# A hybrid decoder step on one core: order of a unit's half products, and raw weight blocks loaded one by one

## The chip, the cores and the metric

The kernel runs on one core of a Trainium2 chip. The time is device time in microseconds (us), from a run on the chip; a run that is profiled as well leaves a trace, from which all rows below come. Matrix products run on TensorE (PE), element-wise work on VectorE (DVE) and ScalarE (ACT), stores are issued from GpSimd (POOL) and nearly all loads from SyncE (SP).

## What is computed

One layer of a hybrid decoder on 1024 new tokens and on 8 single tokens with a state. A combined input projection feeds a gated linear recurrence and a chunked matrix-memory head group; both are merged and projected back. Cut to what matters here:

```
hn = rmsnorm(x, g_norm)                       # (1024, 1024) and (8, 1024)
u = hn @ w_in                                 # w_in (1024, 7176)
xa, za, uq, uk, uv, uo, zb, ui, uf = jnp.split(u, SPLIT_IDX, axis=-1)
yA, hA, bufA = rglru_branch(xa, ...)
hB, C, n, m = mlstm_seq(q, k, v, ig, lf, C0, n0, m0)
...
merged = jnp.concatenate([yA * silu(za), yB * silu(zb)], axis=-1)
x = x + merged @ w_out
y = rmsnorm(x, g_final)
```

The change touches the way in which `u = hn @ w_in` is worked through.

## The kernel before

**Units.** The columns of `w_in` are taken in 14 units of two blocks of 256 columns each (`UNITS`: v0v1, x0y0, q0k0, ... z2z3). Unit 0 is multiplied plainly at the start. For units 1 to 13 the product is a 2 x 2 block product with seven multiplications in place of eight (a Strassen-Winograd scheme): tokens in two halves, the 1024 rows of `w_in` in two halves (b = 0, 1), columns in two blocks (a = 0, 1). `blk(u, a, b)` is one of the four raw weight blocks of a unit; the seven left factors (`cb`) are built once. The products are named by position: `Q_P1, Q_P2, Q_P5, Q_P6, Q_P7, Q_P3, Q_P4 = range(7)`. In the prediction, "first factor" is the weight factor of Q_P1, "second" that of Q_P2, and so on to "seventh", that of Q_P7.

**A product and its halves.** `product(u, q)` makes two half products (s = 0, 1), each of 128 output columns, or, for v and o units, of 256 tokens. Each is a sum of float32 products in three passes (`mm3`, lines 66 to 68: high by high, high by low, low by high): 12 matmuls of 512 columns, or 24 of 256 columns for v and o. Products 1, 6, 7 and 4 add up in one PSUM tile X (tag `kv`, 2 buffers), products 2, and then 5 and 3, in a tile Y (tag `o`, 3 buffers). After each half `evac` reads out: after 1, X is copied by ACT (line 328); after 2, DVE adds Y to the copy (line 331) and the result is stored; 5 (line 335) and 6 (line 338) are copied; 7 (line 341) and 3 (line 345) are added; 4 is copied (line 353) and stored.

**The weight factors.** `prep(u, q)` turns a raw block, or a sum of blocks, into a high and a low part: ACT casts (line 72, `wh`), DVE subtracts (line 73, `wl`). Blocks are summed in place by DVE: at Q_P5 `blk(0,0)` loses `blk(1,0)` (line 279) and `blk(1,0)` gains `blk(1,1)` (line 280); at Q_P6 `blk(1,0)` becomes `blk(1,1) - blk(0,0)` (line 282), and `blk(0,1)` loses it after the split (line 288). The last readers are therefore: of `blk(1,0)` Q_P6, of `blk(0,0)` Q_P7, of `blk(0,1)` Q_P3, of `blk(1,1)` Q_P4. Splits run two products ahead (`LEAD = 2`), in six buffers (`NWS = 6`, three pairs of high and low), so a split can begin when the product three before it has ended. At Q_P5, `dec_unit` first multiplies the 8 single tokens by all four blocks (line 257, 64 small matmuls per unit).

**The raw blocks.** Two tiles of 1 MB (`raw0` for b = 0, `raw1` for b = 1), one buffer each. `load_raw(u, b)` makes a new tile for the unit and issues two loads of 512 KB from SP (line 243), one per column block. The next unit's b = 0 is loaded after Q_P7's split, b = 1 after Q_P4's.

**Beside the products.** Three lists of small steps (`bg`, `rgq`, `dcq`: gates, the recurrence, the single tokens' state, the first chunks of the head group) are popped after each half product by `pop_bg`. In the last unit, `wo_due(q)` puts the steps for the output weights on `bg` after each product. Then comes the second large stage, the output products (`r_prod`) between the chunks.

**What sets the order.** The program text gives priorities. A planner builds each engine's queue at build time: it goes through the instructions with estimated durations and places on each engine the first in program order of those that are ready by its clock. So an instruction can stand ahead of one that is asked for earlier. On the chip each queue runs in its fixed order, and instructions wait on semaphores.

Of the kernel before, what the change touches and what calls it, by code (L numbers as in the profile page):

```python
# [9 lines left out]
F32 = mybir.dt.float32  # L10
# [12 lines left out]
NH = 4  # L23
# [28 lines left out]
def hymba_kernel(  # L52
# [11 lines left out]
    def mm3(out, ah, al, bh, bl, first, last):  # L64

        TE.matmul(out, ah, bh, start=first, stop=False, skip_group_check=True)  # L66
        TE.matmul(out, ah, bl, start=False, stop=False, skip_group_check=True)  # L67
        TE.matmul(out, al, bh, start=False, stop=last, skip_group_check=True)  # L68
# [13 lines left out]
    def ps(tag, shape):  # L82
        return psp.tile(shape, F32, tag=tag, name=f"ps_{tag}", bufs=NBUF.get(tag, 1))
# [17 lines left out]
    def sg(shape, name, dt=F32):  # L101

        return stg.tile(shape, dt, tag="stg", name=name)
# [130 lines left out]
    def load_raw(u, b, parts=(0, 1)):  # L234

        if u >= len(units):
            return
        if (u, b) not in raws:
            raws[u, b] = rawp.tile([P, 4, 512], F32, tag=f"raw{b}", name=f"raw{b}_{u}")
        for a in parts:  # L240
            kind, j = units[u][a]
            c = COL[kind] + j * 256
            ld(raws[u, b][:, :, a * 256:(a + 1) * 256],
               w_in[0, b * HT:(b + 1) * HT, c:c + 256].rearrange("(k p) c -> p k c", p=P))
# [24 lines left out]


    wops = {}

    def blk(u, a, b):
        return raws[u, b][:, :, a * 256:(a + 1) * 256]

    def prep(u, q):
        if q == Q_P5:
            dec_unit(u)
            V.tensor_tensor(blk(u, 0, 0), blk(u, 0, 0), blk(u, 1, 0), op=ALU.subtract)
            V.tensor_tensor(blk(u, 1, 0), blk(u, 1, 0), blk(u, 1, 1), op=ALU.add)  # L280
        if q == Q_P6:
            V.tensor_tensor(blk(u, 1, 0), blk(u, 1, 1), blk(u, 0, 0), op=ALU.subtract)
        src = {Q_P1: (0, 0), Q_P2: (0, 1), Q_P5: (1, 0), Q_P6: (1, 0), Q_P7: (0, 0), Q_P3: (0, 1), Q_P4: (1, 1)}
        hi, lo = ws([P, 4, 256], f"wh{u}_{q}"), ws([P, 4, 256], f"wl{u}_{q}")
        split(hi, lo, blk(u, *src[q]))
        wops[u, q] = hi, lo
        if q == Q_P6:
            V.tensor_tensor(blk(u, 0, 1), blk(u, 0, 1), blk(u, 1, 0), op=ALU.subtract)
        b = {Q_P7: 0, Q_P4: 1}.get(q)
        if b is not None:  # L290
            if u + 1 < len(units):
                load_raw(u + 1, b)
            else:
                if b == 1:
                    r_open(0)

    px = {}

    def product(u, q):

        kind = units[u][0][0]
        wh, wl = wops.pop((u, q))
        bh, bl = cb[q]
        first, last = q in (Q_P1, Q_P2, Q_P5), q in (Q_P2, Q_P3, Q_P4)
        for s in range(2):
            if q == Q_P1:
                px["X", s] = ps("kv", [P, 512])
            if q in (Q_P2, Q_P5):
                px["Y", s] = ps("o", [P, 512])
            X, Y = px["X", s], px.get(("Y", s))  # L310
            out = X if q in (Q_P1, Q_P6, Q_P7, Q_P4) else Y
            if kind in "vo":
                for i in range(2):
                    t = slice((2 * s + i) * P, (2 * s + i + 1) * P)
                    for k in range(4):
                        mm3(out[:, i * 256:(i + 1) * 256], bh[:, k, t], bl[:, k, t], wh[:, k, :], wl[:, k, :],
                            first and i == 0 and k == 0, last and i == 1 and k == 3)
            else:
                c = slice(s * P, (s + 1) * P)
                for k in range(4):  # L320
                    mm3(out, wh[:, k, c], wl[:, k, c], bh[:, k, :], bl[:, k, :], first and k == 0, last and k == 3)
            evac(u, q, s, X, Y)
            yield

    def evac(u, q, s, X, Y):
        if q == Q_P1:
            px["s1", s] = t = sg([P, 512], "s1")
            A.copy(t, X)
        elif q == Q_P2:
            t = px.pop(("s1", s))  # L330
            V.tensor_tensor(t, t, Y, op=ALU.add)
            emit_out(u, 0, 0, s, t)
        elif q == Q_P5:
            px["s5", s] = t = sg([P, 512], "s5")
            A.copy(t, Y)
        elif q == Q_P6:
            px["s2", s] = t = sg([P, 512], "s2")
            A.copy(t, X)
        elif q == Q_P7:
            t = px.pop(("s5", s))  # L340
            V.tensor_tensor(t, t, X, op=ALU.add)
            emit_out(u, 1, 1, s, t)
        elif q == Q_P3:
            t = px.pop(("s2", s))
            V.tensor_tensor(t, t, Y, op=ALU.add)
            emit_out(u, 0, 1, s, t)
        else:
            t = sg([P, 512], "c21")
            o = units[u][1][0] == "o"
            if o:  # L350
                A.activation(t, X, AF.Tanh, scale=0.5)
            else:
                A.copy(t, X)
            emit_out(u, 1, 0, s, t, o)
# [7 lines left out]
    def emit_out(u, a, b, s, t, done=False):  # L362

        kind, j = units[u][a]
        if kind in "xy":
            if a == 1:
                silu2(t)
            stq((d_x, d_y)[a][2 * j + s][:, b * HT:(b + 1) * HT], t)
            return
        if kind in "qk":  # L370
            stq(d_qk[j][(kind == "k") * 2 + s][:, b * HT:(b + 1) * HT], t)
            return
        if kind == "z":
            silu2(t)
            stq(d_zs[2 * j + s, :, b * HT:(b + 1) * HT], t)
            return
        if kind == "o" and not done:
            A.activation(t, t, AF.Tanh, scale=0.5)
        d = {"v": d_v, "o": d_so}[kind][j]
        t0 = b * HT + s * 256  # L380
        stq(d[t0:t0 + 256, :].rearrange("(i p) c -> p i c", p=P), t.rearrange("p (i c) -> p i c", i=2))
# [554 lines left out]
    def dec_rows(half):  # L936

        pvd = ps("s", [NB, 512])
        for m in range(4):
            TE.transpose(pvd[:, m * P:(m + 1) * P], dv[:, 4 * half + m, :], idF)  # L940
        vr = sg([NB, 512], "vr")
        V.tensor_copy(vr, pvd)
        for h in range(2):
            stq(d_dv[2 * half + h], vr[:, h * 256:(h + 1) * 256])
# [457 lines left out]
    def r_open(n):  # L1402

        rring.append(rawp.tile([P, 4, HT], F32, tag="raw1", name="ring0") if n == 0 else slot(5, "ring1", F32))
        for i in range(2 * n, 4):
            r_fetch(4 * n + i)
# [256 lines left out]
            step(Q_P7)  # L1663


    seq = [(u, q) for u in range(1, len(units)) for q in range(7)]
    state = {"prep": 0, "m": False}

    def preps(n):
        while state["prep"] < min(n, len(seq)):  # L1670
            prep(*seq[state["prep"]])
            state["prep"] += 1

    gg = gates()
    bg.extend([lambda: next(gg, None)] * 17 + [rd_open])
    last_u = len(units) - 1
    unit_of = {p: u for u, pair in enumerate(units) for p in pair}
    done_h = [max(unit_of[k, h] for k in "qkv") for h in range(NH)]

    def m_start():  # L1680
        state["m"] = True
        bg.append(m_open1)
        for n in range(NH):
            bg.extend(m_first(n))

    preps(LEAD)
    part = 0
    for n, (u, q) in enumerate(seq):
        preps(n + 1 + LEAD)
        for _ in product(u, q):  # L1690
            pop_bg(2 if u == 1 or u == last_u else 1, 1, part % DEC[1 if u >= DEC[0] else 2] == 1)
            part += 1
        if u == last_u:
            wo_due(q)
        if q == 6:
            for kind, j in units[u]:
                if kind == "x":
                    rg_unit(j)
            for half in range(2):
                if u == max(unit_of["v", 2 * half], unit_of["v", 2 * half + 1], 1):  # L1700
                    bg.append(lambda half=half: dec_rows(half))
            for h in range(NH):
                if done_h[h] == u:
                    bg.append(lambda h=h: dcq.extend(decode_steps(h)))
            if u == last_u - 1:
                dgen = decode_outputs()

                def step():
                    next(dgen, None)
                    run_late()  # L1710
                state["out"] = [step] * 5 + [m_open2]
        if not state["m"] and u > max(done_h) and not (bg or rgq or dcq or late):
            m_start()
        if u == last_u and q == 0:
            if not state["m"]:
                while bg or rgq or dcq or late:
                    pop_bg()
                m_start()
            bg.extend(state["out"])
    while bg or late:  # L1720
        pop_bg()
    with tc.issue_after(lastt[0].ins):
# [102 lines left out]
```

## Time and profile before

| | |
|---|---|
| median of 3 runs | 915.67 us (915.23 to 915.72) |
| the profiled execution | 913.23 us, of which its span 911.3 us |
| granted TensorE clock | 0.999 |
| PE, DVE, ACT busy | 899.6, 739.3, 585.0 us |
| raw block loads (line 243) | 55 loads of 512 KB |

The span runs from the first to the last instruction of the program; a small part of an execution lies around it. Busy times are unions of an engine's instructions; PEld is the loading of matmul weights, which lies beside the matmuls. In a row of the time line the columns are start and duration in us, engine, line of the kernel, operation, output tile, input tiles, shapes and count; in brackets the idle time before it and what ended it. In a row of waits: what waited, for what, us in total, times, longest.

### The profile page before, as it was taken

To read this page: it belongs to the slowest core of one execution; us is meant where nothing else is said; L and a number is where in the kernel's file an instruction comes from. 1 tells how busy PE (TensorE), PEld (TensorE's weight loads), DVE (VectorE), ACT (ScalarE), POOL (GpSimd) and SP (SyncE) were. 2 spreads that over 40 slices of the span, in tenths; PEclk is the share of its full clock that TensorE was granted. 3 is DMA by queue.
4 is the path that set the end of the run, shared out by engine and by line. 5 is a ranking of instruction groups with operands and counts; after the bars stand their busy time and mean duration, and the time that the engine had idled before them with its cause. 6 is when DMAs were issued, how large, how long until landed. Compare 5 with 4: busy or idle time off the path is not lost. (4 is left out here: it accounts for less than half of the span.)

```text
span 911.3 us, 16738 instructions
## 1 busy us (share of the span) xinstructions
PE 899.6 (99%) x5889; PEld 762.3 (84%) x5889; DVE 739.3 (81%) x1528; ACT 585.0 (64%) x1086; POOL 194.2 (21%) x322
## 2 busy tenths in 40 slices
PE   8999999999999999999999999999999999999996
PEld 6997778877788997887789999887788888888886
DVE  6974778979698978789889876679998879888973
ACT  7653446867567776576658775446786568566642
POOL 1111112122222232324332334010111111121120
PEclk9999999999999999999999999999999999999999
DMA  6412447465746566548665747345679888855531
GB/s 200 149 64 92 139 147 250 135 205 187 236 128 221 171 203 204 197 145 266 201 237 184 253 139 244 108 133 191 215 234 259 202 216 296 217 142 180 181 124 67
DMA packets 130493, 167.76 MB, mean 184 GB/s; under 512 B 17596, under 2 KB 98564, under 8 KB 130402
## 3 DMA queue, kind: packets, MB, share of 16 engines
q1 hardware_dynamic: 108790, 103.68, 37.4%
q0 software_dynamic: 21616, 63.02, 20.9%
q8 instruction: 46, 0.75, 0.3%
q14 instruction: 37, 0.30, 0.1%
q10 hardware_dynamic: 4, 0.00, 0.0%
HBM read 108.00 MB, written 62.92 MB: 188 GB/s over the span
## 5 line engine op out<-in xcount | busy, mean ns | idle before, releaser
L72 ACT CAST wh<-raw 128x1024 fp32r<-128x1024 f32 x91 | 95.4, 1049 | 79.5 <-DVE raw L280 21.0
L73 DVE TENSOR_TENSOR wl<-raw,wh 128x1024 fp32r<-128x1024 f32 x91 | 111.1, 1221 | 29.4 <-ACT wh L72 15.8
L66 PE MATMUL ps_kv<-cb_hi,wh 128*128 128x512 f32 x320 | 127.4, 398 | 0.0
L68 PE MATMUL ps_kv<-cb_hi,wl 128*128 128x512 f32 x320 | 125.5, 392 | 0.0
L67 PE MATMUL ps_kv<-cb_lo,wh 128*128 128x512 f32 x320 | 125.2, 391 | 0.0
L66 PE MATMUL ps_o<-cb_hi,wh 128*128 128x512 f32 x240 | 95.2, 397 | 0.0
L68 PE MATMUL ps_o<-cb_hi,wl 128*128 128x512 f32 x240 | 93.7, 391 | 0.0
L67 PE MATMUL ps_o<-cb_lo,wh 128*128 128x512 f32 x240 | 93.6, 390 | 0.0
L66 PEld LDWEIGHTS ps_kv<-cb_hi,wh 128*128 128x128 f32 x320 | 60.1, 188 | 15.9 <-issue 3.1
L68 PEld LDWEIGHTS ps_kv<-cb_hi,wl 128*128 128x128 f32 x320 | 60.1, 188 | 13.4 <-issue 0.6
L67 PEld LDWEIGHTS ps_kv<-cb_lo,wh 128*128 128x128 f32 x320 | 60.1, 188 | 12.7 <-issue 0.8
L66 PE MATMUL ps_kv<-wh,cb_hi 128*128 128x256 f32 x192 | 55.1, 287 | 0.0
L67 PE MATMUL ps_kv<-wl,cb_hi 128*128 128x256 f32 x192 | 54.4, 283 | 0.0
L68 PE MATMUL ps_kv<-wh,cb_lo 128*128 128x256 f32 x192 | 54.3, 283 | 0.0
L66 PEld LDWEIGHTS ps_o<-cb_hi,wh 128*128 128x128 f32 x240 | 45.1, 188 | 10.4 <-issue 0.8
L68 PEld LDWEIGHTS ps_o<-cb_hi,wl 128*128 128x128 f32 x240 | 45.0, 188 | 9.9
L66 PE MATMUL ps_o<-wo,mh 128*128 128x512 f32 (+1 forms) x136 | 53.0, 390 | 0.0
L67 PEld LDWEIGHTS ps_o<-cb_lo,wh 128*128 128x128 f32 x240 | 45.1, 188 | 8.9
L68 PE MATMUL ps_o<-wo,ml 128*128 128x512 f32 (+1 forms) x136 | 51.6, 380 | 0.0
L67 PE MATMUL ps_o<-wo,mh 128*128 128x512 f32 (+1 forms) x136 | 51.5, 379 | 0.0
L66 PE MATMUL ps_o<-wh,cb_hi 128*128 128x256 f32 x144 | 41.0, 284 | 0.0
L67 PE MATMUL ps_o<-wl,cb_hi 128*128 128x256 f32 x144 | 40.7, 283 | 0.0
(559 smaller groups left out, 2603.8 us busy)
## 6 DMA issues: line engine op xcount, KB each, us to landing
raw<-in_w_in_dram SPq DMA_DIRECT2D x55, 512.0 KB
Cb<-in_state_mlstm_C_dram SPq DMA_DIRECT2D x32, 256.0 KB
out_dram<-Cb POOLq DMA_DIRECT2D x32, 256.0 KB, 4.9
qk<-d_qk SPq DMA_DIRECT2D x32, 256.0 KB
ring<-d_ro SPq DMA_DIRECT2D x26, 256.0 KB
d_qk<-s POOLq DMA_DIRECT2D x24, 256.0 KB, 4.8
d_x<-s POOLq DMA_DIRECT2D x16, 256.0 KB, 2.8
zsr<-d_y SPq DMA_DIRECT2D x16, 256.0 KB
```

Source lines behind the costliest of these rows:

```text
L66: TE.matmul(out, ah, bh, start=first, stop=False, skip_group_check=True)
L67: TE.matmul(out, ah, bl, start=False, stop=False, skip_group_check=True)
L68: TE.matmul(out, al, bh, start=False, stop=last, skip_group_check=True)
L72: a = A.copy(hi, src)
L73: V.tensor_tensor(lo, src, hi.bitcast(F32), op=ALU.subtract)
```

## The change

The halves become the unit of order. In units 1 to 12 the second product comes ahead of the first; in the last unit the first stays ahead. Then 5 and 6 as before, the first half of 3, both halves of 7, the second half of 3, and 4. The splits follow the order 2, 1, 5, 6, 7, 3, 4 (1, 2, ... in the last unit), at the halves listed in `PREP`. Whichever of products 1 and 2 is read out first is copied by ACT, the other added by DVE.

One raw tile per b serves all units, and each block of the next unit is loaded on its own, after its last reader's split: `blk(1,0)` after Q_P6, `blk(0,0)` after Q_P7, `blk(0,1)` after Q_P3, `blk(1,1)` after Q_P4. The steps of `wo_due` are put on the list after the halves listed in `DUE`.

```
         if (u, b) not in raws:
-            raws[u, b] = rawp.tile([P, 4, 512], F32, tag=f"raw{b}", name=f"raw{b}_{u}")
+            raws[u, b] = raws[0, b] if (0, b) in raws else rawp.tile([P, 4, 512], F32, tag=f"raw{b}", name=f"raw{b}")
...
+    FREED = {Q_P6: (0, (1,)), Q_P7: (0, (0,)), Q_P3: (1, (0,)), Q_P4: (1, (1,))}
...
-        b = {Q_P7: 0, Q_P4: 1}.get(q)
-        if b is not None:
-            if u + 1 < len(units):
-                load_raw(u + 1, b)
-            else:
-                if b == 1:
-                    r_open(0)
+        if u + 1 < len(units):
+            if q in FREED:
+                load_raw(u + 1, *FREED[q])
+        elif q == Q_P4:
+            r_open(0)
...
-    def product(u, q):
+    def product(u, q, s):
...
-        wh, wl = wops.pop((u, q))
+        wh, wl = wops.pop((u, q)) if s == 1 else wops[u, q]
...
-        if q == Q_P1:
-            px["s1", s] = t = sg([P, 512], "s1")
-            A.copy(t, X)
-        elif q == Q_P2:
-            t = px.pop(("s1", s))
-            V.tensor_tensor(t, t, Y, op=ALU.add)
-            emit_out(u, 0, 0, s, t)
+        if q in (Q_P1, Q_P2):
+            Z = X if q == Q_P1 else Y
+            if ("s1", s) not in px:
+                px["s1", s] = t = sg([P, 512], "s1")
+                A.copy(t, Z)
+            else:
+                t = px.pop(("s1", s))
+                V.tensor_tensor(t, t, Z, op=ALU.add)
+                emit_out(u, 0, 0, s, t)
...
-    seq = [(u, q) for u in range(1, len(units)) for q in range(7)]
+    last_u = len(units) - 1
+    FIRST = lambda u: (Q_P1, Q_P2) if u == last_u else (Q_P2, Q_P1)
+    seq = [(u, q) for u in range(1, len(units)) for q in (*FIRST(u), *range(2, 7))]
...
+    REST = [(Q_P5, 0), (Q_P5, 1), (Q_P6, 0), (Q_P6, 1), (Q_P3, 0), (Q_P7, 0), (Q_P7, 1), (Q_P3, 1), (Q_P4, 0), (Q_P4, 1)]
+    PREP = 0, 2, 4, 6, 8, 11, 12
+    DUE = 1, 3, 5, 7, 10, 12, 13
+
     preps(LEAD)
     part = 0
-    for n, (u, q) in enumerate(seq):
-        preps(n + 1 + LEAD)
-        for _ in product(u, q):
+    for u in range(1, len(units)):
+        for n, (q, s) in enumerate([(q, s) for q in FIRST(u) for s in range(2)] + REST):
+            if n in PREP:
+                preps(7 * (u - 1) + PREP.index(n) + 1 + LEAD)
+            product(u, q, s)
             pop_bg(2 if u == 1 or u == last_u else 1, 1, part % DEC[1 if u >= DEC[0] else 2] == 1)
             part += 1
-        if u == last_u:
-            wo_due(q)
-        if q == 6:
+            if u == last_u and n in DUE:
+                wo_due(DUE.index(n))
+            if n == 13:
...
-        if not state["m"] and u > max(done_h) and not (bg or rgq or dcq or late):
+            if n % 2 and not state["m"] and u > max(done_h) and not (bg or rgq or dcq or late):
...
-        if u == last_u and q == 0:
+            if u == last_u and n == 1:
```

The number of matmuls, casts, sums, loads and stores is the same before and after.

More of the change, by code (lines that the diff above doesn't have):

```diff
@@ L301, in product @@
         kind = units[u][0][0]
-        wh, wl = wops.pop((u, q))
+        wh, wl = wops.pop((u, q)) if s == 1 else wops[u, q]
         bh, bl = cb[q]
         first, last = q in (Q_P1, Q_P2, Q_P5), q in (Q_P2, Q_P3, Q_P4)
-        for s in range(2):
-            if q == Q_P1:
[L307 to L317, printed above, removed]
-            else:
[L319 to L323, printed above, removed]
@@ L325, in evac @@
-    def evac(u, q, s, X, Y):
-        if q == Q_P1:
-            px["s1", s] = t = sg([P, 512], "s1")
-            A.copy(t, X)
-        elif q == Q_P2:
-            t = px.pop(("s1", s))
-            V.tensor_tensor(t, t, Y, op=ALU.add)
-            emit_out(u, 0, 0, s, t)
+        if q == Q_P1:
+            px["X", s] = ps("kv", [P, 512])
+        if q in (Q_P2, Q_P5):
+            px["Y", s] = ps("o", [P, 512])
+        X, Y = px.get(("X", s)), px.get(("Y", s))
+        out = X if q in (Q_P1, Q_P6, Q_P7, Q_P4) else Y
@@ new lines, in product @@
+        if kind in "vo":
+            for i in range(2):
+                t = slice((2 * s + i) * P, (2 * s + i + 1) * P)
+                for k in range(4):
+                    mm3(out[:, i * 256:(i + 1) * 256], bh[:, k, t], bl[:, k, t], wh[:, k, :], wl[:, k, :],
+                        first and i == 0 and k == 0, last and i == 1 and k == 3)
+        else:
+            c = slice(s * P, (s + 1) * P)
+            for k in range(4):
+                mm3(out, wh[:, k, c], wl[:, k, c], bh[:, k, :], bl[:, k, :], first and k == 0, last and k == 3)
@@ L333, in evac @@
+        evac(u, q, s, X, Y)
+    def evac(u, q, s, X, Y):
+        if q in (Q_P1, Q_P2):
[3 more added lines that the diff above has]
+                A.copy(t, Z)
+            else:
+                t = px.pop(("s1", s))
+                V.tensor_tensor(t, t, Z, op=ALU.add)
+                emit_out(u, 0, 0, s, t)
         elif q == Q_P5:
@@ L1675, in hymba_kernel @@
     bg.extend([lambda: next(gg, None)] * 17 + [rd_open])
-    last_u = len(units) - 1
     unit_of = {p: u for u, pair in enumerate(units) for p in pair}
@@ L1691, in hymba_kernel @@
             pop_bg(2 if u == 1 or u == last_u else 1, 1, part % DEC[1 if u >= DEC[0] else 2] == 1)
             part += 1
-        if u == last_u:
-            wo_due(q)
-        if q == 6:
[L1696 to L1711, printed above, removed]
@@ L1712, in hymba_kernel, with step @@
-        if not state["m"] and u > max(done_h) and not (bg or rgq or dcq or late):
-            m_start()
-        if u == last_u and q == 0:
-            if not state["m"]:
-                while bg or rgq or dcq or late:
-                    pop_bg()
-                m_start()
-            bg.extend(state["out"])
+            if u == last_u and n in DUE:
+                wo_due(DUE.index(n))
+            if n == 13:
+                for kind, j in units[u]:
+                    if kind == "x":
+                        rg_unit(j)
+                for half in range(2):
+                    if u == max(unit_of["v", 2 * half], unit_of["v", 2 * half + 1], 1):
+                        bg.append(lambda half=half: dec_rows(half))
+                for h in range(NH):
+                    if done_h[h] == u:
+                        bg.append(lambda h=h: dcq.extend(decode_steps(h)))
+                if u == last_u - 1:
+                    dgen = decode_outputs()
+                    def step():
+                        next(dgen, None)
+                        run_late()
+                    state["out"] = [step] * 5 + [m_open2]
@@ L1720, in hymba_kernel @@
+            if n % 2 and not state["m"] and u > max(done_h) and not (bg or rgq or dcq or late):
+                m_start()
+            if u == last_u and n == 1:
+                if not state["m"]:
+                    while bg or rgq or dcq or late:
+                        pop_bg()
+                    m_start()
+                bg.extend(state["out"])
     while bg or late:
```

## The prediction

> **What bounds the kernel now.** I read the head of the page first: the span, the busy shares, the slices of PE and the granted clock.
>
> ```profile
> span 911.3 us, 16738 instructions
> PE 899.6 (99%) x5889; PEld 762.3 (84%) x5889; DVE 739.3 (81%) x1528; ACT 585.0 (64%) x1086; POOL 194.2 (21%) x322
> PE   8999999999999999999999999999999999999996
> PEclk9999999999999999999999999999999999999999
> ```
>
> PE is busy in 899.6 of 911.3 us at full clock; no other engine comes near. But 81% on DVE is a mean, so I took the busy times by stretches of 20 us (columns: stretch, length, then PE, PEld, DVE, ACT, POOL with instruction counts, clock, DMA share, GB/s). The first and last stretch, one from the middle of the unit loop, and all between 60 and 700 us in which PE is not full:
>
> ```profile
> 0.00:20.00 20.00, 17.12 (x78) 12.67 (x78) 12.15 (x29) 15.09 (x32) 3.22 (x14) 1.00 0.63 198
> 60.00:80.00 20.00, 19.71 (x211) 16.91 (x211) 10.49 (x20) 6.25 (x14) 2.41 (x6) 1.00 0.27 82
> 100.00:120.00 20.00, 19.88 (x143) 15.16 (x142) 17.99 (x63) 9.50 (x21) 4.12 (x10) 1.00 0.36 120
> 360.00:380.00 20.00, 20.00 (x90) 16.49 (x89) 14.95 (x23) 11.99 (x16) 7.57 (x12) 1.00 0.72 248
> 620.00:640.00 20.00, 19.64 (x100) 14.41 (x99) 19.74 (x49) 13.99 (x18) 2.15 (x4) 1.00 0.68 243
> 660.00:680.00 20.00, 19.47 (x109) 16.22 (x108) 19.06 (x41) 17.65 (x37) 3.08 (x6) 1.00 0.77 224
> 900.00:920.00 20.00, 4.36 (x37) 4.15 (x35) 3.19 (x11) 2.24 (x8) 0.00 (x0) 0.90 0.07 27
> ```
>
> The unit loop, which the change reorders, runs from about 72 to 656 us. PE's idle time in the four stretches that belong to it or follow at once is 0.29 + 0.12 + 0.36 + 0.53 = 1.30 us; most of the other idle time lies in the first 20 us and after 900 us, where no line of the change is. The waits of PE name what little there is; of the list, these are the ones after the first 60 us:
>
> ```profile
> PE ps_qp L1298 <- ACT hh L1247: 0.4, 1, 0.4
> PE ps_s L1069 <- DVE dworkb L1067: 0.4, 1, 0.4
> PE ps_tr L257 <- DMA raw<-in_w_in_dram: 0.3, 1, 0.3
> ```
>
> Only the last is a wait for a raw block, 0.3 us in the whole run, and none is for a split weight of the loop or for a PSUM bank to be read out. So the loop is bound by the number of its matmuls, not by operands. Busy is not yet peak, so I looked at the distance between starts:
>
> ```profile
> 199.69 0.39 PE L68 MATMUL ps_kv<-cb_hi,wl 128*128 128x512 f32 x1
> 199.92 0.39 PE L66 MATMUL ps_kv<-cb_hi,wh 128*128 128x512 f32 x1
> 200.15 0.39 PE L67 MATMUL ps_kv<-cb_lo,wh 128*128 128x512 f32 x1
> ```
>
> One starts every 0.23 us: a half product of 12 takes 0.23 x 12 = 2.8 us, a unit of 14 halves some 38 us. The change keeps each matmul, so this sum stays.
>
> **The change part by part.** *Second factor first, units 1 to 12.* The same 24 matmuls in another place. The read-outs trade roles: the second product is now copied by ACT, the first added by DVE.
>
> ```profile
> L328 ACT COPY s<-ps_kv x26: 565/581/594, 80.0 to 617.9; 128x512 f32<-128x512 f32 x26
> L331 DVE TENSOR_TENSOR s<-s,ps_o x26: 677/681/689, 85.2 to 623.7; 128x512 f32<-128x512 f32 x26
> L66 PEld LDWEIGHTS ps_kv<-cb_hi,wh 128*128 128x128 f32 x320 | 60.1, 188 | 15.9 <-issue 3.1 <-ACT xh L813 0.4 <-ACT c L353 0.2
> ```
>
> One copy of 0.58 us and one add of 0.68 us per half before and after, and one store on POOL's queue behind the add (POOL is 21% busy); reading from the other PSUM tile is not a cost that these rows show (the adds and copies elsewhere from either tile differ by under 0.01 us). What it buys is room: bank X of a unit is wanted two halves later after the fourth product's copy. That wait (ACT c, line 353) is 0.2 us on the weight loads in all, so the gain lies between 0 and 0.2 us; I take 0.
>
> *The third factor's first half before the seventh's.* This takes lead away. The splits keep their order and their buffers, so the third factor's split still can't start before the fifth product ends; but its first matmul comes right after the sixth product, where the seventh's starts now: two halves, 5.6 us, sooner. So I compared the end of the third factor's subtraction (line 73) with the seventh product's start (line 66 behind it), in the tightest two units, 1 and 6, and in unit 4, which is near the middle:
>
> ```profile
> 98.00 1.22 DVE L73 TENSOR_TENSOR wl<-raw,wh 128x1024 fp32r<-128x1024 f32 x1 [4.20 <-PE ps_kv L67]
> 98.69 0.50 PE L66 MATMUL ps_kv<-cb_hi,wh 128*128 128x512 f32 x1
> 315.86 1.22 DVE L73 TENSOR_TENSOR wl<-raw,wh 128x1024 fp32r<-128x1024 f32 x1
> 317.70 0.28 PE L66 MATMUL ps_kv<-wh,cb_hi 128*128 128x256 f32 x1
> 225.82 1.22 DVE L73 TENSOR_TENSOR wl<-raw,wh 128x1024 fp32r<-128x1024 f32 x1
> 229.59 0.49 PE L66 MATMUL ps_kv<-cb_hi,wh 128*128 128x512 f32 x1
> ```
>
> Unit 6 keeps 317.70 - 317.08 = 0.6 us, unit 4 229.59 - 227.04 = 2.6 us. Unit 1 is 99.22 - 98.69 = 0.5 us late, since there the buffer itself came free only at the sixth product's end. If it stalls, it costs 0.5 us; if the planner puts a half of the seventh in front, nothing. I take 0.2. The seventh factor gains one half of lead, and bank X is left alone for one half more after the sixth product; nothing waits there now, so that brings 0.
>
> *The next unit's second factor* is split one half later (behind the third product's second half) and wanted at the place of the first factor: one half, 2.8 us, of lead lost where several are there. Cost 0.
>
> *Raw blocks one by one.* The same two loads of 512 KB per K half, issued by SP, each waiting for its own block's last reader. Behind a waiting load stand SP's other loads (gate inputs, state blocks, chunk operands):
>
> ```profile
> SPq L243 <- DVE wl L73: 80.0, 17, 22.8
> ```
>
> Raw loads hold SP's queue for 80 us in all already, and yet PE waits for a load 0.3 us in all. Four shorter holds per unit in place of two cannot bring more than that 0.3; what they could cost is late state or gate inputs, which feed work off the chain that PE fills in as it comes. I take 0. If that cover were gone, a held load would cost its landing time, about 4 us (below), once.
>
> *Last unit.* It keeps first-then-second; its output-weight steps fall due up to one half, 2.8 us, later. The third output weight is the nearest check:
>
> ```profile
> 651.89 1.22 DVE L73 TENSOR_TENSOR wr2l<-ws,wr2h 128x1024 fp32r<-128x1024 f32 x1
> 662.45 0.39 PE L66 MATMUL ps_o<-wr2h,ro 128*128 128x512 f32 x1
> ```
>
> It is ready 662.45 - 653.11 = 9.3 us ahead, so 2.8 us is covered. DVE is nearly full there (19.74 of 20 us), so a new order can move the 0.36 and 0.53 us of PE idle either way: between -0.9 and, by the same size, +0.9; I take 0.
>
> **The sum.** The profiled execution took 913.23 us, 1.93 us around its span. 913.23 + 0.2 (unit 1) - 0.3 (the raw wait) = 913.1. The median of the three runs is 915.67, so 2.4 us above; on its scale 915.67 - 0.1 = 915.6 us. [...]
>
> **The rivals.** *Faster: the broken stretch at the start of unit 1 heals.* There the decode matmuls of line 257 are cut into pieces between the first product's:
>
> ```profile
> 72.45 0.50 PE L66 MATMUL ps_kv<-cb_hi,wh 128*128 128x512 f32 x1
> 72.68 0.98 SPq L243 DMA_DIRECT2D raw<-in_w_in_dram  x2
> 73.12 1.08 PE L257 MATMUL ps_tr<-raw,hnd 128*32 128x128 f32 x32
> 76.74 1.05 ACT L72 CAST wh<-raw 128x1024 fp32r<-128x1024 f32 x1 [3.86 <-DMA raw<-in_w_in_dram]
> 76.76 0.41 PE L257 MATMUL ps_tr<-raw,hnd 128*32 128x128 f32 x4 [0.29 <-DMA raw<-in_w_in_dram]
> 81.64 0.39 PE L66 MATMUL ps_o<-cb_hi,wh 128*128 128x512 f32 x1
> ```
>
> From 72.45 to 81.64 PE needs 9.2 us for 24 matmuls (24 x 0.23 = 5.5 us) and 64 decode matmuls, which at 32 in 1.08 us are 2.2 us: 1.5 us are lost. With all of the 1.30 us idle (0.29 of it in both) the most to win is 2.5 us: 913.2 us, 0.27%. For it speaks that the first product is no longer alone ahead; against, that it needs every loss to go.
>
> *Slower: unit 1 waits for its second factor.* Its block is loaded at 72.68 and lands 4.1 us later, when the cast starts (76.74); the cast ends at 77.79. If the planner keeps the new order to the letter, PE goes from 72.45 to 77.79 with 32 decode matmuls (1.1 us) for work: 5.34 - 1.1 = 4.2 us, so 919.8 us. It decides as soon as the second product's first matmul stands in PE's queue ahead of the first product's. Against it: the planner takes what is ready, as unit 1's first weight cast shows, which ran ahead of casts that the program asks for before it:
>
> ```profile
> 51.55 1.05 ACT L72 CAST wh<-raw 128x1024 fp32r<-128x1024 f32 x1
> 57.27 0.59 ACT L72 CAST b12h<-ps_s 128x512 fp32r<-128x512 f32 x1
> ```
>
> [...]
>
> *Slower: the third factor comes late in many units.* The price is read from the margins: 0.6 to 2.6 us in the units above. If DVE's new order puts it 3.1 us later (some four more DVE instructions of 0.7 us), unit 6 loses 2.5 and a middle unit 0.5 us; 2.5 + 8 x 0.5 = 6.5 us, 922 us. It starts to count at 2.6 us. Against it: the split now stands before work that was before it in need.
>
> *The change does not do what it says:* if a load into a quarter of the kept raw tile still waits for every reader of the tile, or the planner undoes the order of the halves, the time is 915.6 as well.
>
> **How the numbers follow.** A measurement of this kernel tells about 0.2%, 1.8 us, from no change. Forecast, with the change without effect: 0.70, own range 914.4 to 916.9 (all 0.9 us of the last unit and the 0.3 and 0.5 us either way). Faster by over 0.2%: 0.14. Unit 1 waiting: 0.08; third factor late: 0.08. The range 913.0 to 918.4 takes in the faster case and small stalls of either slower one.
>
> **What would show it.** Right: PE still at 20.00 in the stretches from 120 to 600 us, starts 0.23 us apart, no wait of PE on wl or raw over 0.5 us; raw loads (line 243) issued singly, in four places per unit. The first product ahead of the second at 72 us in spite of the program. Wrong: PE idle at 72 to 78 us, or at the third product's start in unit after unit; or a busy sum on PE that moves by over 2 us, for which I have no cause.

## The result: slower by 0.9%

| | before | after |
|---|---|---|
| median of 5 runs, us | 915.72 (915.23 to 916.05) | 923.53 (922.43 to 925.41) |
| ratio, 95% interval | | 1.0088 (1.0075 to 1.0102) |
| the profiled execution, us | 913.23 | 923.49 |

The prediction (915.6, range 913.0 to 918.4) was wrong: the time is outside it, on the slower side. The head of the page of after:

```profile
span 921.7 us, 16758 instructions
PE 901.7 (98%) x5889; PEld 763.1 (83%) x5889; DVE 740.3 (80%) x1528; ACT 585.1 (63%) x1086; POOL 194.7 (21%) x322
PE   8998999999999999999999999999999999999996
```

The same 5889 matmuls are there, and PE's busy time has grown by 2.1 us only. The span has grown by 10.4 us, so some 8 us are new idle time of PE. (The medians are 7.8 us apart and the two profiled executions 10.3, since that of before lies 2.4 us under its median; what follows accounts for the profiled pair.) The busy times by stretches of after show where (columns as in the prediction):

```profile
60.00:80.00 20.00, 16.61 (x199) 14.61 (x198) 10.25 (x20) 6.86 (x13) 2.42 (x6) 0.91 0.26 82
140.00:160.00 20.00, 19.12 (x83) 15.18 (x82) 16.31 (x30) 13.86 (x19) 4.62 (x8) 1.00 0.84 276
360.00:380.00 20.00, 18.45 (x81) 14.94 (x80) 17.10 (x30) 11.34 (x15) 7.19 (x11) 1.00 0.73 240
460.00:480.00 20.00, 19.32 (x153) 15.60 (x146) 11.68 (x19) 9.98 (x13) 3.90 (x7) 1.00 0.55 193
480.00:500.00 20.00, 19.00 (x157) 18.05 (x157) 16.96 (x30) 13.10 (x19) 8.92 (x13) 1.00 0.63 216
```

The stretch of unit 1's start has lost 3.1 us of PE (16.61 where before has 19.71), and four places in the middle of the loop, where before ran full, lack 0.7 to 1.6 us each. The waits of PE in after give names to them:

```profile
PE ps_tr L257 <- DMA raw<-in_w_in_dram: 2.4, 1, 2.4
PE ps_o L68 <- DVE wl L73: 2.1, 2, 1.5
...
PE ps_o L66 <- ACT wh L72: 1.0, 2, 0.7
PE ps_qp L1019 <- DVE qC L1014: 1.0, 1, 1.0
...
PE ps_kv L66 <- DVE s L340: 0.7, 1, 0.7
```

One wait for a raw block, two for the third factor's low part (wl), one for the add of the seventh product (line 340). To see how they add up, take the start of each unit, the first product matmul of the unit in the two timelines; the difference is what has been lost up to there:

| unit | 1 | 2 | 3 | 7 | 8 | 9 | 10 | 11 | 12 | 13 |
|---|---|---|---|---|---|---|---|---|---|---|
| before, us | 72.45 | 119.11 | 161.00 | 339.04 | 383.03 | 426.12 | 470.00 | 517.42 | 564.76 | 611.31 |
| after, us | 76.69 | 122.64 | 165.86 | 344.20 | 390.03 | 433.08 | 477.95 | 526.63 | 574.82 | 621.37 |
| lost, us | 4.24 | 3.53 | 4.86 | 5.16 | 7.00 | 6.96 | 7.95 | 9.21 | 10.06 | 10.06 |

Unit 1 starts 4.2 us late, and 3.5 us of that are left when unit 2 starts; units 2, 7, 9, 10 and 11 lose 0.9 to 1.8 us each; the last unit loses nothing. The two numbers of unit 1 are not of the same work: in after, 36 more of the decode matmuls, some 1.2 us (32 take 1.08 us), stand ahead of its first product.

**Unit 1.** The time line of after at its start, on PE and then on ACT:

```profile
72.17 1.08 PE L257 MATMUL ps_tr<-raw,hnd 128*32 128x128 f32 x32 [0.36 <-ACT Z L260]
75.61 0.41 PE L257 MATMUL ps_tr<-raw,hnd 128*32 128x128 f32 x4 [2.36 <-DMA raw<-in_w_in_dram]
76.69 0.80 PE L66 MATMUL ps_o<-cb_hi,wh 128*128 128x512 f32 x1 [0.66 <-ACT wh L72]
75.59 1.99 ACT L72 CAST wh<-raw 128x1024 fp32r<-128x1024 f32 x2 [3.48 <-DMA raw<-in_w_in_dram]
```

PE does its 32 decode matmuls and stops: the next thing in its queue needs the block of the second factor, which comes at 75.6. The first product, whose block was there, stands behind. On ACT the casts stand in the same new order, two in a row at 75.59; in before the first factor's cast ran at 51.55. The stretch of 4 us right after, in the same columns as the stretches above, shows a granted clock of 0.57:

```profile
76.00:80.00 4.00, 3.34 (x34) 2.25 (x32) 3.33 (x4) 1.58 (x2) 0.00 (x0) 0.57 0.13 36
```

A matmul of line 67 takes 0.63 us there (at 77.28) and 0.39 us at 80.49, where the clock is back at 1.00 (80 to 84 us). As an estimate from the row above, 3.34 us of matmuls at 0.57 would have taken 1.4 us less at the full clock, so most of the 2.1 us by which PE's busy time grew lies here.

**Units 2 to 11.** Unit 9 shows how such a wait comes about. Time lines of after, on SP, ACT, DVE and PE:

```profile
459.32 0.38 SPq L243 DMA_DIRECT2D raw<-in_w_in_dram  x1
460.42 1.67 SPq L966 DMA_DIRECT2D Cb<-in_state_mlstm_C_dram  x2
468.22 0.72 ACT L987 ACTIVATE Cb<-Cb,dGI 128x512 f32<-128x512 f32 x1 [5.74 <-DMA Cb<-in_state_mlstm_C_dram]
468.98 0.88 DVE L989 SCALAR_TENSOR_TENSOR Cb<-vbc,kw,Cb 128x256 f32<-128x256 f32 x2 [4.48 <-ACT Cb L987]
472.38 0.68 DVE L340 TENSOR_TENSOR s<-s,ps_kv 128x512 f32<-128x512 f32 x1
473.11 0.50 PE L66 MATMUL ps_kv<-cb_hi,wh 128*128 128x512 f32 x1 [0.68 <-DVE s L340]
```

Read it downward. A state of a single token (Cb) is loaded behind a raw block. ACT stands 5.74 us at the step that scales it, DVE stands 4.48 us at the step behind it. When both go on, DVE's add of the seventh product is late, behind this step and three others that DVE runs first (468.98 to 472.38 us), and PE, which wants that bank back, waits 0.68 us. PE never waits for the state itself. In unit 7 of after the same happens with the row that is added to the state (vbc), and there the third factor's subtraction (line 73) comes late:

```profile
366.41 0.88 DVE L989 SCALAR_TENSOR_TENSOR Cb<-vbc,kw,Cb 128x256 f32<-128x256 f32 x2 [2.08 <-DMA vbc<-d_dv]
369.78 1.22 DVE L73 TENSOR_TENSOR wl<-raw,wh 128x1024 fp32r<-128x1024 f32 x1
371.05 0.50 PE L68 MATMUL ps_o<-cb_hi,wl 128*128 128x512 f32 x1 [1.55 <-DVE wl L73]
```

### The profile page after: what moved, and what is told of

Read it like the earlier page. It is cut to its first block, busy times and chain, and to the rows that moved or that the text cites. A ratio compares the mean times of both kernels' runs of the same rounds, so it can differ in the third digit from the quotient of the medians.

```text
span 921.7 us, 16758 instructions
## 1 busy us (share of the span) xinstructions
PE 901.7 (98%) x5889; PEld 763.1 (83%) x5889; DVE 740.3 (80%) x1528; ACT 585.1 (63%) x1086; POOL 194.7 (21%) x322
## 5 line engine op out<-in xcount | busy, mean ns | idle before, releaser
L987 ACT ACTIVATE Cb<-Cb,dGI 128x512 f32<-128x512 f32 x32 | 23.0, 721 | 30.0 <-DMA Cb<-in_state_mlstm_C_dram 29.9
```

Source lines behind the costliest of these rows:

```text
L987: A.mul(C, C, dGI[:, b, h:h + 1])
```

## The experiments

The change falls into four parts: **A**, unit 1 begins with the second factor; **B**, units 2 to 12 do; **C**, the third factor's halves around the seventh's; **D**, raw blocks one by one. Each edit turns parts of after back. First A; then A and B; then C; then D:

```
-    FIRST = lambda u: (Q_P1, Q_P2) if u == last_u else (Q_P2, Q_P1)
+    FIRST = lambda u: (Q_P1, Q_P2) if u in (1, last_u) else (Q_P2, Q_P1)
...
-    FIRST = lambda u: (Q_P1, Q_P2) if u == last_u else (Q_P2, Q_P1)
+    FIRST = lambda u: (Q_P1, Q_P2)
...
-    REST = [(Q_P5, 0), (Q_P5, 1), (Q_P6, 0), (Q_P6, 1), (Q_P3, 0), (Q_P7, 0), (Q_P7, 1), (Q_P3, 1), (Q_P4, 0), (Q_P4, 1)]
-    PREP = 0, 2, 4, 6, 8, 11, 12
-    DUE = 1, 3, 5, 7, 10, 12, 13
+    REST = [(Q_P5, 0), (Q_P5, 1), (Q_P6, 0), (Q_P6, 1), (Q_P7, 0), (Q_P7, 1), (Q_P3, 0), (Q_P3, 1), (Q_P4, 0), (Q_P4, 1)]
+    PREP = 0, 2, 4, 6, 8, 10, 12
+    DUE = 1, 3, 5, 7, 9, 11, 13
...
-            raws[u, b] = raws[0, b] if (0, b) in raws else rawp.tile([P, 4, 512], F32, tag=f"raw{b}", name=f"raw{b}")
+            raws[u, b] = rawp.tile([P, 4, 512], F32, tag=f"raw{b}", name=f"raw{b}_{u}")
...
-    FREED = {Q_P6: (0, (1,)), Q_P7: (0, (0,)), Q_P3: (1, (0,)), Q_P4: (1, (1,))}
+    FREED = {Q_P7: (0, (0, 1)), Q_P4: (1, (0, 1))}
```

For A alone, `FIRST` takes the second factor first where `u == 1` only. All of these runs in one table, each against the kernel before on the same chip:

| run | parts left in | median, us | before, us | ratio (95%) |
|---|---|---|---|---|
| all_undone | none | 914.57 | 914.79 | 1.0000 (0.9990 to 1.0010) |
| u1_second | A | 919.48 | 914.40 | 1.0053 (1.0036 to 1.0069) |
| only_second | B | 917.24 | 914.79 | 1.0024 (1.0014 to 1.0033) |
| only_third | C | 921.09 | 914.79 | 1.0072 (1.0047 to 1.0097) |
| only_loads | D | 919.59 | 914.79 | 1.0045 (1.0029 to 1.0061) |
| u1_rest | B, D | 921.10 | 914.43 | 1.0066 (1.0045 to 1.0088) |
| old_rest | A, B, D | 922.32 | 914.43 | 1.0082 (1.0064 to 1.0101) |
| u1_first | B, C, D | 920.23 | 914.43 | 1.0068 (1.0048 to 1.0089) |
| old_loads | A, B, C | 926.12 | 914.43 | 1.0122 (1.0098 to 1.0145) |
| after | A, B, C, D | 923.53 | 915.72 | 1.0088 (1.0075 to 1.0102) |

**First four runs: one part turned back, or two.** What was expected of u1_first, old_rest, old_loads and u1_rest, in this order:

> Unit 1 takes its first factor ahead of its second again, all else as after the change. Theory (three places that add up): the 4.2 us by which unit 1 starts late go, less the 0.7 us that it won back by its end: about 3.5 us under the changed kernel, 920.0 us (919.3 to 920.7), first matmul of unit 1 at 72.5 us and no wait of PE on a raw block over 0.5 us. Rival (the loads one by one hold unit 1 back): 923 us or more, and PE still waits 2.4 us for a raw block.

> Both halves of the seventh product ahead of both of the third again, second factor still first, loads still one by one. Theory: the two waits on the third factor's low part (2.1 us of PE idle, 2.9 us in the starts of units 3 and 8) and the 0.84 us on bank X in unit 9 go: 919 to 920 us. Rival (the planner's new order of the side work costs it, whatever the halves): 922 to 924 us, with waits of PE on qC, xh or OC as long as now.

> Raw blocks loaded as before: a new tile per unit, two blocks after the seventh's split and two after the fourth's; the order of the halves as changed. Theory: the loads cost and bring nothing, 923.5 us (922.5 to 924.5). Rival (the loads are the cause): 919 us or less, with unit 1 back at 72.5 us.

> First factor first in unit 1 and the seventh's halves ahead of the third's; second factor first in units 2 to 12 and loads one by one stay. Theory: both losses go and add up: 915.5 to 917.5 us. Rival (side work reshuffled): 918 us or more, PE idle between 460 and 580 us as in the changed kernel.

With A turned back (u1_first), unit 1's first matmul is at 72.33 again, and the median is inside its band. But the kernel before ran 1.3 us faster on that chip than beside after: each against its own before, u1_first costs 5.8 us and after 7.8, so A is worth 2.0 us here and not 3.5, and the two intervals overlap. The theories of the other three missed. Without C the waits on wl were gone, but others had come; old_rest and u1_rest took the times of their rivals, without most of the waits that the rivals named. Without D the time rose, which neither side had. So what is left outside unit 1 doesn't belong to one part that one could take out.

**One part alone, and none.**

> The changed kernel's code with all three parts turned back: first factor first in every unit, the seventh factor's halves before the third's, raw blocks loaded in pairs into a new tile per unit. What is left of the change is only how the loops are written. Theory (the loss lies in the three parts): as the kernel before, 914.5 to 916.5 us, and TensorE without a wait over 0.35 us between 80 and 600 us. Rival (the rewritten loops themselves move background work): 918 us or more.

> Only the raw loads one by one stay; the order of the products is that of before. Theory L (single raw loads stand on SP's queue between the loads of the states, and hold up ScalarE's and VectorE's state steps until TensorE waits): 918 to 921 us, with waits of TensorE of 0.5 to 2 us on ScalarE's or VectorE's copies and casts in the units that update states. Rival S (the second factor's place in units 2 to 12 uses up the room): 914.5 to 916.5 us and no such wait.

> Only the second factor's product ahead of the first's stays, in units 2 to 12 (unit 1 and the last begin with the first factor). Theory L: 914.5 to 916.5 us. Rival S: 918 to 921 us, with waits on ScalarE or VectorE at the first products or at the states' steps.

> Only the third factor's halves around the seventh's stay. The third factor's cast and difference have two halves of lead in place of four, 5.6 us in place of 11.2. Theory L: the lead is mostly enough without the single loads, 915 to 917 us, with at most two waits on wl of together up to 1.5 us. Rival (the third factor's shortened lead alone is enough): 918 us or more.

> Only unit 1 begins with the second factor; everything else as before the change. Theory (TensorE stands at the second factor's first matmul until the late half block has come, and then runs at the lower clock): 3.5 to 4.5 us of unit 1's start, 917.8 to 919.3 us. Rival (the loss of unit 1 is used up by waits that before has later anyway): at most 916.5 us.

With nothing left in, the rewritten loops are as fast as before: the loss is in the four parts. (Its profiled execution was the slowest of its ten, 916.99 us, and does show waits of 0.4 to 0.9 us at 475, 501 and 560 us, so the second half of that expectation missed.) Each part alone costs something: 5.1, 2.5, 6.3 and 4.8 us by the medians of A, B, C and D, 18.7 us together. All four cost about 8: they don't add up. A lies 0.2 us above its band, with unit 1's first product 4.3 us late (76.77 for 72.45 us); put on top of B and D it costs 1.2 us (old_rest against u1_rest) and not 5.1, so other losses cover most of it there. D came out as theory L had it, though its longest wait is of another kind (below). B lies between L and S, and for C theory L fell: 921.1 us without the single loads. The rival had the time of C but not the reason: no wait on wl is in the list of that trace, and its longest is on ACT's copy of line 352 (1.91 us, unit 10).

Of D alone, the stall of unit 2, on SP, ACT and PE:

```profile
132.25 0.39 SPq L243 DMA_DIRECT2D raw<-in_w_in_dram  x1
133.72 0.42 SPq L966 DMA_DIRECT2D Cb<-in_state_mlstm_C_dram  x1
135.84 0.79 SPq L966 DMA_DIRECT2D Cb<-in_state_mlstm_C_dram  x1
139.86 0.72 ACT L987 ACTIVATE Cb<-Cb,dGI 128x512 f32<-128x512 f32 x1 [2.51 <-DMA Cb<-in_state_mlstm_C_dram]
142.15 0.72 ACT L987 ACTIVATE Cb<-Cb,dGI 128x512 f32<-128x512 f32 x1 [1.56 <-DMA Cb<-in_state_mlstm_C_dram]
144.19 0.58 ACT L337 COPY s<-ps_kv 128x512 f32<-128x512 f32 x1
144.82 0.50 PE L66 MATMUL ps_kv<-cb_hi,wh 128*128 128x512 f32 x1 [1.89 <-ACT s L337]
```

And SP in before at the same place:

```profile
132.22 0.90 SPq L967 DMA_DIRECT2D Cb<-in_state_mlstm_C_dram  x2
135.37 0.34 SPq L745 DMA_DIRECT2D xs<-d_x  x1
136.51 1.06 SPq L243 DMA_DIRECT2D raw<-in_w_in_dram  x2
```

Before, both states were asked for at 132.2 and the raw blocks 4 us later. With single loads the first raw block goes ahead, as its own reader has ended, and the second state is asked for 3.6 us later. ACT stands there twice, the copy of the sixth product's half is late, and PE waits 1.89 us. The unit loses 3.9 us (45.81 us for 41.89), twice the wait, for in the stretch behind it the clock is at 0.57:

```profile
145.50:149.50 4.00, 4.00 (x13) 3.14 (x12) 3.17 (x7) 3.88 (x6) 1.42 (x2) 0.57 0.70 210
```

The same trace has a second stall, in unit 11, and its wait is PE's longest in the loop. On ACT, DVE and PE:

```profile
559.81 0.41 ACT L72 CAST vh<-vt 128x256 fp32r<-128x256 f32 x1 [4.26 <-DMA vt<-d_v]
561.53 0.26 ACT L909 ACTIVATE dxc<-dxc 128x64 f32<-128x64 f32 x1
562.56 0.22 DVE L912 TENSOR_TENSOR OC<-dgr 128x64 f32<-128x64 f32 x1
562.92 1.01 PE L925 MATMUL ps_s<-idF,OC 128*20 128x128 f32 x4 [2.46 <-DVE OC L912]
```

The same two steps in before, on ACT:

```profile
555.38 0.26 ACT L910 ACTIVATE dxc<-dxc 128x64 f32<-128x64 f32 x1
560.22 0.41 ACT L72 CAST vh<-vt 128x256 fp32r<-128x256 f32 x1 [1.35 <-DMA vt<-d_v]
```

ACT stands 4.26 us at the cast of a chunk's value rows (vt), and a step of the single tokens' recurrence that PE's transposes need is behind it. In before these two steps stand the other way round. The rows come no later than there (559.81 for 560.22 us, though the unit itself runs 3.8 us later), so here the planned order of ACT's queue makes the stall, and no late load. Unit 11 loses 3.8 us too, and the clock behind the wait is 0.66 (563 to 567 us). Together the two stalls make up the 7.6 us by which unit 13 starts late in this trace.

Of A alone, unit 10 has a stall too, although nothing near it is changed; ACT and PE:

```profile
468.56 0.72 ACT L987 ACTIVATE Cb<-Cb,dGI 128x512 f32<-128x512 f32 x1 [4.54 <-DMA Cb<-in_state_mlstm_C_dram]
477.27 0.62 ACT L812 CAST xh<-xc 64x512 fp32r<-64x512 f32 x1 [3.08 <-DVE na L846]
478.95 0.59 ACT L352 COPY c<-ps_kv 128x512 f32<-128x512 f32 x1
479.59 0.39 PE L66 MATMUL ps_kv<-wh,cb_hi 128*128 128x256 f32 x1 [1.66 <-ACT c L352]
```

The same steps in before, on ACT:

```profile
462.08 0.72 ACT L988 ACTIVATE Cb<-Cb,dGI 128x512 f32<-128x512 f32 x1 [2.16 <-DMA Cb<-in_state_mlstm_C_dram]
470.80 0.62 ACT L813 CAST xh<-xc 64x512 fp32r<-64x512 f32 x1 [3.08 <-DVE na L847]
472.48 0.59 ACT L353 COPY c<-ps_kv 128x512 f32<-128x512 f32 x1
```

The queue is the same, and in before too ACT waits 2.16 us for that state. With unit 1 late by 4 us, SP's order around there is still that of before, but the state comes 6.5 us later (468.56 for 462.08): 2.4 us more than the shift, and the copy that PE needs is behind it. So at this place before has no room to speak of; the wait ends just in time.

**Three guesses at one cause.** First third_early2, the third factor's lead given back (its split ahead of the seventh's, with C alone); then loads_pool, raw loads on GpSimd's queue (with D alone); then loads_b1, the first two blocks as a pair again (with D alone):

```
-    seq = [(u, q) for u in range(1, len(units)) for q in (*FIRST(u), *range(2, 7))]
+    seq = [(u, q) for u in range(1, len(units)) for q in (*FIRST(u), Q_P5, Q_P6, Q_P3, Q_P7, Q_P4)]
...
-            ld(raws[u, b][:, :, a * 256:(a + 1) * 256],
+            (ld if u < 2 else stq)(raws[u, b][:, :, a * 256:(a + 1) * 256],
...
-    FREED = {Q_P6: (0, (1,)), Q_P7: (0, (0,)), Q_P3: (1, (0,)), Q_P4: (1, (1,))}
+    FREED = {Q_P7: (0, (0, 1)), Q_P3: (1, (0,)), Q_P4: (1, (1,))}
```

> The third factor's halves around the seventh's, as in the run with that part alone, but its cast and difference made ahead of the seventh's, so that it has four halves of lead again; the seventh's has three. Theory A (the third's lead of two halves was what cost 6.3 us): 915 to 917.5 us. Theory B (the room of the banks and the thinner leads of whatever comes after it cost it: bank X is to be free one half sooner after the seventh product, the next unit's first split one half later): 919 us or more, with TensorE's waits on ps_kv and not on wl.

> Raw loads one by one alone, as in the run with that part alone, but from unit 2 on issued by GpSimd's queue and not SP's. Theory C (a raw load that waits for its reader stands on SP's queue ahead of the states' and the gates' loads, and these come late): under 917 us, ScalarE's idle time ahead of the states' scaling back from 26 us to under 18 us. Theory D (not the queue but the bandwidth of the earlier raw loads makes the states' loads late): 918 us or more and over 22 us of that idle time. If GpSimd's stores fall behind a waiting raw load, waits on the staging buffers of the products' results would show instead.

> Raw loads one by one alone, but the first block's two halves again loaded together after the seventh factor's split; only the second block's two are one by one. Theory (the half block that is loaded after the sixth factor's split comes ahead of the states' loads and makes unit 2's stall): no wait on ScalarE's copy of the sixth product near 143 us, 914.5 to 917 us. Rival (any order of loads other than before's moves the states' loads): 918 us or more, with the waits elsewhere.

third_early2 took 922.96 us (ratio 1.0102, 1.0053 to 1.0152): theory A fell, more lead for the third factor didn't help, and the stalls lay elsewhere, the longest 1.86 us on DVE's add of line 330 in unit 8. Theory B's time was met, but only one of its long waits was on ps_kv. loads_pool took 921.09 (1.0072, 1.0057 to 1.0087), with 28.4 us of ACT's idle time at the state steps: theory C fell, D's two numbers were met, though nothing shows that bandwidth is the reason. Unit 2's stall went, and unit 10 got two of 1.0 and 1.9 us. loads_b1 took 917.43 (1.0035, 1.0022 to 1.0048) and didn't do what it says: SP issues raw at 132.15, the states at 133.61 and 135.73, raw at 136.50, the same as with D alone. It may be that with one tile for all units a load can go as soon as its own quarter is free, and that the planner takes it forward whatever the list says; that was not tried. So it decides nothing about the order, but it is a second run of the same stalls: in unit 11 PE waits 1.80 us, again behind ACT's cast of vt, and in unit 2 1.71 us, with this stretch after it:

```profile
145.30:150.00 4.70, 4.70 (x21) 3.57 (x20) 3.82 (x7) 4.54 (x7) 1.43 (x2) 1.00 0.73 224
```

Here the clock stayed at 1.00, and unit 2 lost 2.3 us and not 3.9.

**Taking the wait away.** The last six were to show whether the waiting state steps carry the loss. In the first four these steps work on a tile of zeros; in the last two they read a constant and write two tiles in turn:

```
-                A.mul(C, C, dGI[:, b, h:h + 1])
+                A.mul(Cx, Cx, dGI[:, b, h:h + 1])
...
-                    V.scalar_tensor_tensor(C[:, kb, :], vb_, st["kw"][:, kb, b:b + 1], C[:, kb, :],
+                    V.scalar_tensor_tensor(Cx[:, kb, :], Cx[:, 1 - kb, :], st["kw"][:, kb, b:b + 1], Cx[:, kb, :],
...
+                C = p2.tile([P, 2, 256], F32, tag="Cx", name="Cx", bufs=2)
+                A.mul(C.rearrange("p a (r c) -> p (a r) c", r=2), idF.unsqueeze(1).to_broadcast([P, 4, P]), dGI[:, b, h:h + 1])
```

> The changed kernel, but ScalarE's and VectorE's state steps compute on a tile of zeros that is always there, in place of the loaded state and the loaded row: the same instructions of the same sizes, the same loads and stores, only no wait for the loads. The new states are left out (the old ones are stored), and the decode outputs with them. Theory E (ScalarE and VectorE stand at a state's load with TensorE's copies behind them): 5 us of the loss in units 2 to 10 go, unit 1's 4.3 stay: 917.5 to 920 us. Theory F (the order of the products leaves too little room whatever the loads do): 922 us or more.

> As the run before, and unit 1 begins with the first factor. The new states are left out. Theory E: 914.5 to 917 us (920.2 with the waits); at most a wait near 560 us for another load is left. Theory F: 919 us or more.

> All three parts turned back, and the state steps without the wait. The new states are left out. Theory E and F alike: 913.5 to 915 us, since TensorE has almost no wait there to lose. If it falls by more, the states' loads cost the kernel before something too.

> The third factor's halves around the seventh's alone, and the state steps without the wait. The new states are left out. Theory E: 914.5 to 917 us in place of 921.1. Theory F: 919 us or more.

> The changed kernel with unit 1 as before (920.2 us), whose state steps read a constant and write two tiles in turn, which are stored; the states are still loaded, and the decode products read them as loaded; the rows of the values are not loaded (32 loads of 128 KB less). Left out: the new states and the decode outputs. Theory E (the waits for the states' loads carry the loss of units 2 to 10): at most 1.5 us above its control. Theory F (the order of the products leaves too little room whatever the loads do): 4 to 6 us above its control, as with the waits.

> Control: all three parts turned back, the state steps as in the run before. Left out: the new states and the decode outputs. Both theories: 913 to 915 us, TensorE without a wait over 0.5 us between 80 and 600 us. Should this one stall too, the two are compared by their waits and not by their times.

All four of the first set became much slower, the control as well: 933.51, 928.82, 934.25 and 934.29 us, where before took 914.91, so their numbers tell neither theory from the other. The wait had not gone; it had another name. The waits of ACT in nw_before:

```profile
ACT Cx L989 <- DVE Cx L991: 22.4, 9, 7.4
```

Each step now waited for DVE's step on the same tile. The second set: 922.59 (nw3_u1, ratio 1.0086, 1.0072 to 1.0100) and 924.65 us (nw3_before, 1.0107, 1.0088 to 1.0126). ACT waited for the store of the tile two steps back; the waits of ACT and PE in nw3_before:

```profile
ACT Cx L986 <- DMA out_dram<-Cx: 23.3, 12, 5.9
PE ps_kv L66 <- ACT s L337: 4.5, 3, 2.0
PE ps_kv L66 <- ACT c L352: 3.1, 2, 1.6
```

So neither set took the wait away, and what the loss would be without it stays open. They show something else. In both controls the order of the products is that of before, and none of the changed parts is in. When ACT stands at its state steps for up to 5.9 or 7.4 us at a time, where before has 2.7 at most, PE stalls on ACT's copies (7.6 us in nw3_before), and the kernel is as slow as the changed one or slower. nw3_u1, with B, C and D in it, was no slower than its control; theory F had asked for 4 to 6 us.

## Why the prediction was wrong

- **Second factor first, cost 0.** This failed, in both places. In unit 1 the slower rival happened, and the sign set for it, PE idle between 72 and 78 us, is in the trace: 3.4 us (0.36 + 2.36 + 0.66) where before has 0.29. That the start is 4.24 us late where 4.2 was forecast is luck in part: the block came 1.15 us sooner than the price had it (cast at 75.59 for 76.74), and 1.2 us of decode matmuls moved ahead of the first product; the lower clock (0.57 from 76 to 80 us), left out of that price, adds some 1.4 us (the estimate above). What failed was the argument that gave the rival 0.08, that the planner takes what is ready. PE's queue kept the programmed order of the two products, and the planner put the second factor's cast ahead of the first's on ACT too. The early cast in before, taken as evidence, was first in the program among the casts of products. Why the planner left the first factor's cast, which in before ran at 51.55, until 75.59 is not shown. In units 2 to 12 the part costs 2.5 us, which no long wait of its profiled execution explains; the longest in the loop is 0.5 us, and that execution, of 915.52 us, is the fastest of its ten.
- **The faster rival's mechanism** is not shown. From its first product to that of unit 2, unit 1 is 0.7 us shorter (45.95 for 46.66 us), but 1.2 us of decode matmuls are no longer in that stretch.
- **The third factor's first half, 0.2.** Mis-sized, and for a reason that the step didn't hold. The margins came from one trace, of units 1, 4 and 6; after's waits on wl are in units 2 and 7, behind state steps that wait. Nor was it the lead alone: given back, it changed nothing for the better. The price of the rival, 922, came near the measured 921.1 of the part alone by luck: no wait on wl is in that trace's list.
- **Bank X.** The step said that it is left alone for one half more after the sixth product. It missed that after the seventh it is wanted one half sooner (two halves where there were three); that is the 0.68 us wait on line 340 in unit 9.
- **Raw blocks one by one, 0.** This failed: 4.8 us alone. The clause that failed is that late state inputs feed work that PE fills in as it comes. The state steps stand on ACT's and DVE's queues, and behind them stand the copies and subtractions that PE needs: in unit 2 of D alone ACT stood 2.51 and 1.56 us at two of them, and the copy that PE wanted ran after both, at 144.19 us. The price set for a held load, 4 us once for its landing, came near the 3.9 us of unit 2 by luck: those are a wait of 1.89 us and a lower clock behind it (0.57 over 4 us), and D alone paid such a price twice, in unit 11 for a changed order of ACT's queue.
- **Last unit and matmul spacing** held: unit 13 is 44.8 us long before and after, and in after too the matmuls of a half product start 0.23 us apart (209.81, 210.04, 210.27 us).
- **The chance of 0.70** rested on PE's list of waits, which was nearly empty. The waits one step further back were in before's trace as well, 17.6 us of ACT's idle time at the state steps, and weren't looked at.

What stays open is how the loss outside unit 1 divides between late loads, thinner leads and new orders of the side work. Shown are the chains in units 2, 7, 9 and 10 of single traces, each led by a waiting state step, the one in unit 11 of D alone, led by a cast that waits, and that longer waits at the state steps stall before's order too. That nothing else is in it is not shown: units 10 and 11 of after lost 1.3 and 0.9 us at steps whose chains weren't followed. No run was clearly faster than the kernel before.

## What to carry to other kernels

An engine without waits is not an engine with room: look one step back, at what the engines that feed it wait for, and how far those waits are from reaching it, in every unit and in more than one trace. A load that feeds only side work is on the path once its first reader stands on an engine's queue ahead of something the bound engine needs: in unit 2 of D alone such readers held ACT for 2.51 and 1.56 us, and PE waited 1.89 us for the copy behind them. And where a rival decides by what a planner does, the planned order of the queues should be read, not argued.

## What was not expected of the hardware

The TensorE clock fell after short waits, and not each time. After waits of 1.89 us (D alone, unit 2) and 1.79 us (B and D) the granted clock was 0.57 and 0.59 over some 4 us, and after 2.46 us (D alone, unit 11) it was 0.66; after 1.71 us (loads_b1, unit 2) and 1.91 us (C alone, unit 10) it was 1.00. Over the whole profiled execution the mean granted clock was 0.995 in D alone and 0.998 in loads_b1, which waits at both places too (1.71 and 1.80 us). The stall in unit 2 cost 3.9 us where the wait was 1.89 us and the clock 0.57, and 2.3 us where the wait was 1.71 us and the clock 1.00. The runs scatter as well: D alone gave four runs of 917.2 to 918.1 us and four of 921.1 to 921.5, while the kernel before stayed within 913.5 to 915.8 on that chip. The mean granted clock was 0.998 in each of the first four, and 0.995 to 0.997 in the others. So the clock may be what parts the two groups; only one run of them, of 921.51 us, has a trace, so that is not shown.
